# Late gates in single file, their stores issued by ScalarE, and the scan's first weights asked for at its opening

## The chip, the cores and the metric

One core of a Trainium2 chip runs the whole program. The metric is the device time of one execution in microseconds (us). The core has five engines that each work through their own list of instructions in order: PE (TensorE, the matrix unit), DVE (VectorE), ACT (ScalarE), POOL (GpSimd) and SP (SyncE, which here only issues DMAs). An engine waits where the next instruction of its list needs something that another engine or a DMA has not delivered; the instructions behind it wait too.

## The reference

One layer of a hybrid network: an FFN, a token mixer, and a second FFN, each with a layer norm. 128 context tokens and 1024 latent tokens (1152 in all, worked on as three column blocks of 384) with a width of 1024. The mixer makes one wide projection; its first columns feed a bidirectional recurrent branch with states (the scan), the next 512 a branch of centred means over windows of 2, 4, 8 and 16 tokens (pooling), and the last 2048 are the logits of two gates, which merge the branches:

```
proj = h @ p['w_mix_in']
ps = proj[..., :SHIFT_W]
pool_in = proj[..., SHIFT_W:SHIFT_W + D_B]
gate_logits = proj[..., SHIFT_W + D_B:]
...
s_final, y = lax.scan(_rwkv7_step, s0.astype(f32), xs)
...
y_a = y.astype(h.dtype) @ p['w_o_rwkv']
u = _centred_pool_residual(pool_in).reshape(b, t, POOL_GROUPS, POOL_GROUP_DIM)
u = jnp.einsum('btgc,gcd->btgd', u, p['w_pool']).reshape(b, t, D_B) * p['pool_scale']
y_b = u @ p['w_o_pool']
gate_a = jax.nn.sigmoid(gate_logits[..., :D_MODEL])
gate_b = jax.nn.sigmoid(gate_logits[..., D_MODEL:])
return (gate_a * y_a + gate_b * y_b) @ p['w_out'], s_final
```

## The kernel before

The program runs through stages: first FFN, the mixer's projections and preparations, the scan, the second FFN. The change lies where the projections end and the scan begins.

**Weights.** A product in float32 accuracy is made of three matmuls, of a high and a low half of each operand (L158 to L160). The class `Weights` fetches a weight block of 128x1024 by a DMA of SP into `wr` (two buffers), ACT casts it to the high half `wh` (L125), and DVE or POOL by turns subtracts to give the low half `wl` (L127); of the late gates the even ones have their `wl` from DVE, the odd ones from POOL. `wh` and `wl` have two buffers each here, so the cast for gate n waits until PE has read gate n-2.

**Late gates (L883 to L889).** Eight of the sixteen gate blocks, numbers 0 to 7, are made before the scan. Each has three column blocks b, each a gemm of 24 matmuls into PSUM, a sigmoid on ACT into `ga` (two buffers), and a store of 192 KB by SP into `gab`. The gates go in pairs: both gates' blocks 2 and 1 by turns, then both blocks 0. Each pair so needs the second gate's weights after two of its six gemms and frees the first gate's weights only after five.

**Beside them.** In the same part of the program two solves (`Solve`, index 0 and 1) prepare the scan: DVE works through 31 pairs of a multiply (L776, `pr`) and a subtraction (L778, `Wd`) and two transposes (L786 `Xi`, L787 `Yt`); of solve 0, PE then makes small products `ph` (L808) in the middle of the gates' matmuls, with copies on ACT (L802, L815 to L823). POOL and DVE make the pooling means (L905 to L911), stored as `u` by SP. The order of each engine's list here is made by the scheduler of the framework, from the program's text and its model of durations; so a change of the loop moves instructions on all engines.

**The scan's opening.** From `manual_schedule` on, the order is that of the text. Per step, PE makes `pa` (L1070) and `pt` (L1078), DVE masks `pa` to `LM` (L1072), ACT copies `pt` to `KBT` (L1080), then `xy`, `Xs`, `us`, `sp`. Into the gaps a generator, the filler, puts the rest of the gates and the pooling projection (`proj`, L936 to L940, and `pw`), one matmul at a time. Its weights come by `Halves`: loads of 128x512 by SP (L140, `wr<-in_w_pool`, `wr<-in_w_mix`), casts on ACT (L149), subtractions on POOL (L150). Its first two loads `uf` (L988) and its first weights are issued when the generator is first advanced, which is inside scan step 0, behind the loads of states (L1039), `ak` and `Gq`. The buffers of the scan stage lie where those of the late gates lay, so they come free with the last gates.

Of the kernel before, what the change touches and what calls it, by code (L numbers as in the profile page):

```python
# [9 lines left out]
F32 = mybir.dt.float32  # L10
# [7 lines left out]
P = 128  # L18
TAIL = 4
MODS = 3  # L20
EARLY = 8
# [14 lines left out]
BN = 384  # L36
# [25 lines left out]
def tile_step(ctx: ExitStack, tc: tile.TileContext, I: dict, O: dict):  # L62
    nc = tc.nc
    V, A, G, S, PE = nc.vector, nc.scalar, nc.gpsimd, nc.sync, nc.tensor
# [532 lines left out]
    with pool("mp", 4, psum=True) as psum, pool("ma", 2, psum=True) as paux, \  # L597
# [275 lines left out]
        with pool("m2") as pl:  # L873
            sols = [Solve(i) for i in range(9)]
            for k in range(22):
                sols[0].at(k)
            for k in range(13):
                sols[1].at(k)
            for s_, cs_ in enumerate(((0, 1), (1, 0), (2, 17))):
                load_ak(s_, cs_, 0)  # L880
            load_v(0, 0, (0, 1))
            load_v(1, 0, (2, 17))
            for n0 in range(0, EARLY, 2):  # L883
                for n, b in ((n0, 2), (n0, 1), (n0 + 1, 2), (n0 + 1, 1), (n0, 0), (n0 + 1, 0)):
                    ps = psum.tile([P, 512], F32, name="pm", tag="mm")
                    gemm(ps, W.get(27 + n), hs, b)
                    ga = pl.tile([P, 8, 64], F32, name="ga", tag="ga", bufs=2).rearrange("p h v -> p (h v)")[:, :BN]
                    A.activation(ga, ps[:, :BN], AF.Sigmoid)
                    S.dma_start(gab_d[n][b][:, 0, :], ga)  # L889
            for g, w in enumerate(WINDOWS):  # L890
                hw = w // 2
                base = (hw, TC + 3 * hw)
                invc = pl.tile([P, T], F32, name="invc", tag="invc", bufs=1)
                S.dma_start(invc, I["invc"][g].unsqueeze(0).broadcast_to([P, T]))
                pp = pl.tile([P, T + 32], F32, name="pp", tag="pp", bufs=1)
                G.memset(pp[:, 0:hw], 0.0)
                G.memset(pp[:, hw + TC:TC + 3 * hw], 0.0)
                G.memset(pp[:, T + 3 * hw:T + 4 * hw], 0.0)
                S.dma_start(pp[:, hw:hw + TC], pin_d[g][:, 0:TC])
                S.dma_start(pp[:, TC + 3 * hw:T + 3 * hw], pin_d[g][:, TC:])  # L900
                n, st, src = T + 4 * hw, 1, pp
                while st < w:
                    n -= st
                    dst = pl.tile([P, T + 32], F32, name="ws", tag="ws", bufs=2)
                    G.tensor_tensor(dst[:, :n], src[:, :n], src[:, st:st + n], ALU.add)  # L905
                    src = dst
                    st *= 2
                for o, ln, bs in ((0, TC, base[0]), (TC, T - TC, base[1])):
                    m = src[:, bs - hw:bs - hw + ln]
                    V.tensor_tensor(m, m, invc[:, o:o + ln], ALU.mult)  # L910
                    G.tensor_tensor(m, m, pp[:, bs:bs + ln], ALU.subtract)  # L911
                    S.dma_start(u_d[g][:, o:o + ln], m)
# [39 lines left out]
    def filler(psG):  # L952
        u = 0

        def nextw(look=2):
            nonlocal u
            u += 1
            return GW.get(u - 1, look)

        hh = hs[0]  # L960
        for b in range(NB):
            sl = slice(b * BN, (b + 1) * BN)
            if b:
                for n in (6, 7):
                    yield from back(*prev, n)
            u2 = [sg.tile([P, 4, BN], F32R, name="u2", tag=f"u2{k}", bufs=1) for k in range(2)]
            gts = {}

            def proj(n):
                ps = psG.tile([P, 512], F32, name="pm", tag="mm")  # L970
                for hf in range(2):
                    w = nextw()
                    yield from steps3(ps[:, :BN], [(w3(w[0], i), w3(w[1], i), hh[0][:, 4 * hf + i, :], hh[1][:, 4 * hf + i, :]) for i in range(4)],
                                      hf == 0, hf == 1)
                gts[n] = sg.tile([P, BN], F32, name="gt", tag="gt", bufs=3)
                A.activation(gts[n], ps[:, :BN], AF.Sigmoid)

            def back(b, u2, gts, n):
                w = nextw()
                ps = psG.tile([P, 512], F32, name="pb", tag="mm")  # L980
                yield from steps3(ps[:, :BN], [(w3(w[0], i), w3(w[1], i), u2[0][:, i, :], u2[1][:, i, :]) for i in range(4)])
                gt = gts.pop(n)
                V.tensor_tensor(gt, gt, ps[:, :BN], ALU.mult)
                later(gab_d[n][b][:, 1, :], gt)

            def load_u(g):
                t = sg.tile([P, BN], F32, name="uf", tag="uf", bufs=2)
                S.dma_start(t, u_d[g][:, sl])  # L988
                return t

            ufs = [load_u(0), load_u(1)]
            wp = nextw()
            first = chain(proj(0), proj(1))
            next(first)
            yield
            for g in range(4):
                uf = ufs[g]
                uh, ul = [sg.tile([P, BN], F32R, name="us", tag=f"us{k}", bufs=1) for k in range(2)]
                A.copy(uh, uf)
                G.tensor_tensor(ul, uf, uh.bitcast(F32), ALU.subtract)  # L1000
                for _ in range(PWGAP):
                    next(first)
                    yield
                ps = psG.tile([P, 512], F32, name="pw", tag="mm")
                yield from steps3(ps[:, :BN], [(w3(wp[0], g), w3(wp[1], g), uh, ul)])
                A.activation(uf, ps[:, :BN], AF.Copy, scale=pcol("pool_scale", g))
                split(uf, u2[0], u2[1], g, G)
                if g < 2:
                    ufs.append(load_u(g + 2))
            yield from first  # L1010
            for n in range(2, 8):
                yield from proj(n)
                if n == 7 and b < 2:
                    hh = [hpA.tile([P, KT, BN], F32R, name="hg", tag="hb") for k in range(2)]
                    for ks in (slice(0, 4), slice(4, 8)):
                        for k in range(2):
                            S.dma_start(hh[k][:, ks].bitcast(F32), h2_d[b + 1][k][:, ks])
                yield from back(b, u2, gts, n - 2)
            prev = (b, u2, gts)
        for n in (6, 7):  # L1020
            yield from back(*prev, n)

    with pool("s1") as pl, pool("gn") as gn, pool("spa", 2, psum=True) as psA, pool("spx", 1, psum=True) as psX, \
# [12 lines left out]
        def init_ctx(hb):  # L1036
            for d in range(2):
                G.memset(states[0, d], 0.0)
                S.dma_start(states[1, d], I["state"][d][:, 4 * hb:4 * hb + 4])  # L1039
# [164 lines left out]
        n = len(steps)  # L1204
        fl = filler(psG)
# [25 lines left out]
            fill(k)  # L1231

        with tc.manual_schedule(engines={PE.engine, V.engine, A.engine, G.engine, S.engine}):
            init_ctx(0)
            for s in range(3):
                pre(s)
                if s % 2 == 0:
                    load(s // 2)
            for s in range(2):
                for d in range(2 - s):  # L1240
                    pre_lm(s, d)
                    pre_kb(s, d)
            for s in range(n):
                if s == 18:
                    init_ctx(1)
                main(s)
                if s % 2 and s + 3 < n:
                    load((s + 3) // 2)
                if s + 1 < n:
                    pre_kb(s + 1, 1)  # L1250
                if s + 2 < n:
                    pre_lm(s + 2, 0)
                slot_work(s, 2)
                fill(2)
                if s + 2 < n:
                    pre_kb(s + 2, 0)
                hb, j = s // 18, s % 18
                if j == 1:
                    for d in range(2):
                        S.dma_start(O["st"][d][:, 4 * hb:4 * hb + 4], states[0, d])  # L1260
                for tt in range(9):
                    if (1 if tt == 0 else max(max(c, 19 - c) for c in (2 * tt, 2 * tt + 1))) == j:
                        waitgn.append(group_norm(hb, tt))
            while gns or waitgn:
                if waitgn:
                    gns.append(waitgn.pop(0))
                flush()
                drive(gns)
                for _ in range(10):
                    next(fl, None)  # L1270
            for _ in fl:
                pass
            flush()
# [177 lines left out]
```

## Time and profile before

| | us |
|---|---|
| median of 3 runs | 3419.12 |
| fastest, slowest of them | 3418.05, 3431.08 |
| the profiled execution | 3418.87 |
| its span in the trace | 3416.8 |
| PE busy in it | 3206.2 (94%) |
| DVE, ACT, POOL busy | 2002.7, 1187.2, 1308.0 |

The span runs from the first to the last instruction of the trace. PE's weight loads (PEld) overlap its matmuls. In lines of the timeline the bracket at the end is the idle time of that engine just ahead of the instruction, and what ended it; the releaser is inferred, and of several it is the latest one that the profile shows. PE's granted clock is given as a share of 2.4 GHz: 1.00 is that level, and 0.50 is the lower level of 1.2 GHz.

### The profile page before, as it was taken

To read this page: it belongs to the slowest core of one execution; us is meant where nothing else is said; L and a number is where in the kernel's file an instruction comes from. 1 tells how busy PE (TensorE), PEld (TensorE's weight loads), DVE (VectorE), ACT (ScalarE), POOL (GpSimd) and SP (SyncE) were. 2 spreads that over 40 slices of the span, in tenths; PEclk is the share of its full clock that TensorE was granted. 3 is DMA by queue.
4 is the path that set the end of the run, shared out by engine and by line. 5 is a ranking of instruction groups with operands and counts; after the bars stand their busy time and mean duration, and the time that the engine had idled before them with its cause. 6 is when DMAs were issued, how large, how long until landed. Compare 5 with 4: busy or idle time off the path is not lost.

```text
span 3416.8 us, 62644 instructions
## 1 busy us (share of the span) xinstructions
PE 3206.2 (94%) x25742; PEld 3044.4 (89%) x25742; DVE 2002.7 (59%) x3300; ACT 1187.2 (35%) x2006; POOL 1308.0 (38%) x1026
## 2 busy tenths in 40 slices
PE   7999999999999999888799889988999999999997
PEld 7999999999888888578688778878999999999996
DVE  6888633347537788866377777544574322323467
ACT  4111111125434444542255555544353111111133
POOL 5111211126446765754121452267763111111144
PEclk9999999999999999789899999999999999999998
DMA  6344211123455545556255566556541111111142
GB/s 238 131 137 137 91 44 38 50 75 130 170 171 161 171 151 160 159 167 206 89 176 163 173 189 210 167 165 222 201 154 38 38 49 38 50 38 45 55 134 95
DMA packets 271533, 433.29 MB, mean 127 GB/s; under 512 B 77840, under 2 KB 173584, under 8 KB 270224
## 3 DMA queue, kind: packets, MB, share of 16 engines
q1 hardware_dynamic: 271248, 429.30, 38.9%
q8 instruction: 202, 3.31, 0.4%
q14 instruction: 83, 0.68, 0.1%
HBM read 311.29 MB, written 96.53 MB: 119 GB/s over the span
## 4 chain that ended last, share of the span: by engine, by line
PE 60%; DVE 16%; DMA 9%; issue 5%; POOL 5%; ACT 3%; SPq 2%; DVEq 0%; POOLq 0%; ACTq 0%
PE pg L159 9%; PE pg L160 9%; PE pg L158 9%; PE po L159 4%; PE po L158 4%; PE po L160 4%; PE pm L158 2%; PE pm L160 2%; PE pm L159 2%; DVE wl L127 2%; PE pa L1070 2%; PE xy L1101 2%; DVE Wd L778 2%; DVE fm L403 2%; DVE pr L776 2%
## 5 line engine op out<-in xcount | busy, mean ns | idle before, releaser
L125 ACT CAST wh<-wr 128x1024 fp32r<-128x1024 f32 x270 | 280.5, 1049 | 800.9 <-PE po L159 432.6
L127 POOL TENSOR_TENSOR wl<-wr,wh 128x1024 fp32r<-128x1024 f32 x117 | 289.2, 2472 | 490.5 <-ACT wh L125 490.2
L295 POOL TENSOR_TENSOR gl<-sg,gh 128x384 fp32r<-128x384 f32 x132 | 157.6, 1194 | 784.0 <-ACT gh L294 784.0
L158 PE MATMUL po<-gh,wh 128*128 128x384 f32 x1056 | 357.3, 338 | 6.4 <-ACT gh L294 2.9
L159 PE MATMUL pg<-h1l,wh 128*128 128x384 f32 x1056 | 355.7, 337 | 7.5 <-POOL h1l L167 7.4
L159 PE MATMUL po<-gl,wh 128*128 128x384 f32 x1056 | 358.1, 339 | 3.6 <-POOL gl L295 3.6
L160 PE MATMUL po<-gh,wl 128*128 128x384 f32 x1056 | 356.4, 337 | 0.0
L158 PE MATMUL pg<-h1h,wh 128*128 128x384 f32 x1056 | 356.4, 337 | 0.0
L160 PE MATMUL pg<-h1h,wl 128*128 128x384 f32 x1056 | 354.5, 336 | 0.0
L158 PE MATMUL pg<-h3h,wh 128*128 128x384 f32 x1056 | 353.6, 336 | 0.0
L160 PE MATMUL pg<-h3h,wl 128*128 128x384 f32 x1056 | 353.5, 335 | 0.0
L159 PE MATMUL pg<-h3l,wh 128*128 128x384 f32 x1056 | 353.2, 335 | 0.0
L127 DVE TENSOR_TENSOR wl<-wr,wh 128x1024 fp32r<-128x1024 f32 x153 | 222.4, 1458 | 218.4 <-ACT wh L125 218.4
L160 PE MATMUL pm<-h2h,wl 128*128 128x384 f32 x936 | 328.2, 351 | 16.7 <-DVE wl L127 16.7
L292 DVE TENSOR_TENSOR sg<-sg,pg 128x384 f32<-128x384 f32 x132 | 73.0, 553 | 459.7 <-PE pg L160 453.6
L158 PE MATMUL pm<-h2h,wh 128*128 128x384 f32 x936 | 328.6, 351 | 0.9 <-ACT pads L442 0.9
L159 PE MATMUL pm<-h2l,wh 128*128 128x384 f32 x936 | 328.0, 350 | 0.0
L312 DVE SCALAR_TENSOR_TENSOR ac<-po,modh,ac 128x384 f32<-128x384 f32 (+1 forms) x352 | 172.9, 514 | 96.5 <-PE po L160 96.5
L403 DVE SCALAR_TENSOR_TENSOR fm<-fm 128x512 f32<-128x512 f32 x224 | 181.2, 809 | 54.7 <-DMA fm<-in_w_mod 51.5
L159 PEld LDWEIGHTS pg<-h1l,wh 128*128 128x128 f32 x1056 | 199.4, 189 | 10.9 <-POOL h1l L167 10.2
L158 PEld LDWEIGHTS po<-gh,wh 128*128 128x128 f32 x1056 | 199.6, 189 | 9.7 <-ACT gh L294 3.6
L160 PEld LDWEIGHTS pm<-h2h,wl 128*128 128x128 f32 x936 | 182.1, 195 | 24.0 <-DVE wl L127 17.3
(287 smaller groups left out, 7471.5 us busy)
## 6 DMA issues: line engine op xcount, KB each, us to landing
wr<-in_ffn_in SPq DMA_DIRECT2D x120, 512.0 KB
ak<-ak SPq DMA_DIRECT2D x48, 768.0 KB
ak<-ak SPq DMA_DIRECT2D x72, 512.0 KB
wr<-in_ffn_out SPq DMA_DIRECT2D x60, 512.0 KB
fm<-in_w_mod SPq DMA_DIRECT2D x112, 256.0 KB
wr<-in_w_mix SPq DMA_DIRECT2D x39, 512.0 KB
sh<-pads SPq DMA_DIRECT2D x108, 130.0 KB
wr<-in_w_mix SPq DMA_DIRECT2D x48, 256.0 KB
```

Source lines behind the costliest of these rows:

```text
L125: A.copy(h[:, :w], r[:, :w])
L127: e.tensor_tensor(l[:, :w], r[:, :w], h[:, :w].bitcast(F32), ALU.subtract)
L158: PE.matmul(ps, wh, xh, start=first and k == 0, stop=False)
L159: PE.matmul(ps, wh, xl, start=False, stop=False)
L160: PE.matmul(ps, wl, xh, start=False, stop=last and k == n - 1)
L292: lastv[0] = V.tensor_tensor(sg, sg, pu[:, :BN], ALU.mult)
L295: G.tensor_tensor(gs[j, b][1][:, sl], sg, gs[j, b][0][:, sl].bitcast(F32), ALU.subtract)
L312: lastv[0] = V.scalar_tensor_tensor(accs[b][:, n, s0:s1], po[:, s0:s1], modh[:, gate_i // 4, n, g:g + 1], accs[b][:, n, s0:s1], ALU.mult, ...
L403: V.scalar_tensor_tensor(jk, w, 1.0, silc[:, s, hf * 512:hf * 512 + 512], ALU.mult, ALU.mult, accum_out=part[:, kt, s, hf:hf + 1])
L776: V.tensor_tensor(o, Wd[:, 0:k + 1, k].unsqueeze(2).broadcast_to([P, k + 1, 31 - k]), Gq[:, k, k + 1:32].unsqueeze(1).broadcast_to([P, k + ...
L778: V.tensor_tensor(Wd[:, 0:k + 1, k + 1:32], Wd[:, 0:k + 1, k + 1:32], o, ALU.subtract)
L1070: PE.matmul(pa[e][:, i, :], ak[es, i, 128:256], ak[es, i, 0:128], start=True, stop=True)
```

## The change

Three edits. The late gates are listed in single file: gates 0 to 5 one after the other, each with its blocks 2, 1, 0, and only gates 6 and 7 still as a pair. The tile `ga` is [128, 384] with three buffers, where it was cut from a larger one with two, and its store is issued by ACT (`A`) where SP (`S`) issued it. The filler stops (`yield`) in its first pass once its first two `uf` loads and first weights are issued, and is advanced to that point ahead of the scan's first instructions.

```diff
@@ -880,13 +880,14 @@
             load_v(0, 0, (0, 1))
             load_v(1, 0, (2, 17))
-            for n0 in range(0, EARLY, 2):
-                for n, b in ((n0, 2), (n0, 1), (n0 + 1, 2), (n0 + 1, 1), (n0, 0), (n0 + 1, 0)):
+            late = [(n, b) for n in range(EARLY - 2) for b in (2, 1, 0)]
+            for n, b in late + [(n, b) for bs in ((2, 1), (0,)) for n in (EARLY - 2, EARLY - 1) for b in bs]:
+                if True:
                     ps = psum.tile([P, 512], F32, name="pm", tag="mm")
                     gemm(ps, W.get(27 + n), hs, b)
-                    ga = pl.tile([P, 8, 64], F32, name="ga", tag="ga", bufs=2).rearrange("p h v -> p (h v)")[:, :BN]
+                    ga = pl.tile([P, BN], F32, name="ga", tag="ga", bufs=3)
                     A.activation(ga, ps[:, :BN], AF.Sigmoid)
-                    S.dma_start(gab_d[n][b][:, 0, :], ga)
+                    A.dma_start(gab_d[n][b][:, 0, :], ga)
@@ -990,6 +991,8 @@
             ufs = [load_u(0), load_u(1)]
             wp = nextw()
+            if b == 0:
+                yield
             first = chain(proj(0), proj(1))
@@ -1231,6 +1234,7 @@
         with tc.manual_schedule(engines={PE.engine, V.engine, A.engine, G.engine, S.engine}):
+            next(fl)
             init_ctx(0)
```

The scheduler's lists show what moves. On DVE, at the start of solve 0, `wl_13927` is the low half of gate 2's weights before, `wl_13955` the same after; `pr` and `Wd` are the pairs of the solve, `ws` a pooling mean. Before:

```order
L127 TENSOR_TENSOR wl_13430<-wr_13427,wh_13429 128x1024
...
L776 TENSOR_TENSOR pr_13551<-Wd_13549,Gq_13540 128x31
...
L778 TENSOR_TENSOR Wd_13549<-Wd_13549,pr_13551 128x7x25
L776 TENSOR_TENSOR pr_13551<-Wd_13549,Gq_13540 128x8x24
L127 TENSOR_TENSOR wl_13927<-wr_13924,wh_13926 128x1024
L778 TENSOR_TENSOR Wd_13549<-Wd_13549,pr_13551 128x8x24
```

After:

```order
L127 TENSOR_TENSOR wl_13430<-wr_13427,wh_13429 128x1024
L911 TENSOR_TENSOR ws_14583<-ws_14583,invc_14575 128x128
L911 TENSOR_TENSOR ws_14583<-ws_14583,invc_14575 128x1024
L127 TENSOR_TENSOR wl_13955<-wr_13952,wh_13954 128x1024
L776 TENSOR_TENSOR pr_13551<-Wd_13549,Gq_13540 128x31
```

Gate 2's low half has moved ahead of the solve's first pair. In the same way gate 4's now stands inside solve 0, ahead of the pair 24x8 (before: behind solve 0's transposes), and gate 6's in the middle of solve 1, behind the pair 17x15 (before: ahead of its last pair). The pairs themselves keep their order. On PE the first products `ph` of solve 0 stand behind 12 gemms and 8 matmuls of the gates (296 matmuls), where they stood behind 11 gemms and 17 matmuls (281).

On SP, where the gates end and the scan opens (`Sc` are the states of the scan, `ak` operands of a later step, `Gq` and `Wd` those of solve 2). Before:

```order
L889 DMA gab_0_113<-ga 128x384
L889 DMA gab_0_116<-ga 128x384
L1039 DMA Sc_14683<-in_state 128x256
...
L862 DMA ak_14790<-ak_2_85 128x1024
L765 DMA Gq<-qd_0_1_162 16x1x1024 x2
...
L988 DMA uf<-u_191 128x384
L988 DMA uf<-u_192 128x384
L140 DMA wr<-in_w_pool 128x512
L140 DMA wr<-in_w_mix 128x512 x5
```

After:

```order
L913 DMA u_194<-ws 128x1024
L989 DMA uf<-u_191 128x384
L989 DMA uf<-u_192 128x384
L140 DMA wr<-in_w_pool 128x512
L140 DMA wr<-in_w_mix 128x512 x4
L1042 DMA Sc_14683<-in_state 128x256
...
L862 DMA ak_14818<-ak_2_85 128x1024
L765 DMA Gq<-qd_0_1_162 16x1x1024 x2
```

The stores of the gates are gone from SP, and the filler's loads stand ahead of the states, `ak` and `Gq`. The second `uf` load waits for the last matmul of gate 7, since its buffer lies where that gate's weights lay.

On ACT, in the same place. Before:

```order
L888 ACTIVATE ga<-pm 128x384 x7
L1080 COPY KBT_14709<-pt 128x512
L1080 COPY KBT_14729<-pt 128x512
L1080 COPY KBT_14749<-pt 128x512
L1111 COPY Xs<-xy 64x2x4x64 x2
L149 CAST wh<-wr 128x512 x4
```

After:

```order
L889 ACTIVATE ga<-pm 128x384
L890 DMA gab_0_113<-ga 128x384
L889 ACTIVATE ga<-pm 128x384
L890 DMA gab_0_116<-ga 128x384
L149 CAST wh<-wr 128x512 x3
L1083 COPY KBT_14737<-pt 128x512
L1083 COPY KBT_14757<-pt 128x512
L1083 COPY KBT_14777<-pt 128x512
L1114 COPY Xs<-xy 64x2x4x64 x2
L149 CAST wh<-wr 128x512
```

Each sigmoid is now followed by its store in ACT's own list, and three of the filler's casts stand ahead of the `KBT` copies. On POOL three of the subtractions L150 likewise stand ahead of the two memsets of the states (L1038 before). Each DMA issue, on either engine, also waits for an earlier DMA, since both take their completion semaphores by turns from the same eight: a store on ACT can so wait for a load that SP issued, and the other way round. At the passage from the scan to the second FFN a few loads, casts and subtractions also change places.

## Rows read from the trace of the kernel before

**Rows 1.** The windows view: each stretch's length, busy time of PE, PEld, DVE, ACT and POOL (with instructions), the granted clock, the DMA engines' busy share and GB/s.

```profile
1560.00:1580.00 20.00, 12.91 (x61) 12.91 (x62) 19.04 (x31) 2.09 (x5) 8.05 (x7) 0.74 0.92 313
...
1620.00:1640.00 20.00, 10.85 (x63) 10.53 (x62) 18.87 (x39) 3.48 (x5) 6.30 (x3) 0.84 0.16 59
...
1680.00:1700.00 20.00, 8.62 (x90) 7.17 (x92) 0.50 (x2) 6.16 (x9) 5.91 (x5) 0.57 0.59 163
```

**Rows 2.** The waits of PE from 1520 to 1720 us: what waited for what, us in total, times, the longest.

```profile
PE pm L160 <- DVE wl L127: 16.7, 2, 9.1
PE pm L936 <- ACT wh L149: 12.8, 1, 12.8
PE ph L808 <- DVE Yt L787: 2.0, 1, 2.0
PE pm L940 <- POOL wl L150: 0.9, 1, 0.9
```

**Rows 3.** The timeline of PE: start, duration, line, operation. First the wait for gate 2's low half, then `ph` of solve 0, then the wait for gate 6's low half, then the last gate's matmuls and the scan's opening.

```profile
1567.09 0.69 PE L160 MATMUL pm<-h2h,wl 128*128 128x384 f32 x1 [7.54 <-DVE wl L127]
...
1595.16 0.24 PE L808 MATMUL ph<-Yt,Nt 32*32 32x32 f32 x2 [2.03 <-DVE Yt L787]
...
1639.88 0.69 PE L160 MATMUL pm<-h2h,wl 128*128 128x384 f32 x1 [9.15 <-DVE wl L127]
...
1643.88 0.36 PE L160 MATMUL pm<-h2h,wl 128*128 128x384 f32 x1
...
1665.93 0.34 PE L160 MATMUL pm<-h2h,wl 128*128 128x384 f32 x1
1666.90 1.16 PE L1070 MATMUL pa<-ak 64*128 64x128 f32 x16 [0.63 <-ACT ga L888]
...
1673.49 2.00 PE L1101 MATMUL xy<-Sc,ak 64*128 64x64 f32 x32
...
1676.50 1.16 PE L1070 MATMUL pa<-ak 64*128 64x128 f32 x16
1690.48 0.69 PE L936 MATMUL pm<-h2h,wh 128*128 128x384 f32 x1 [12.82 <-ACT wh L149]
```

**Rows 4.** The timeline of DVE: solve 0's first pair, gate 2's low half, the subtraction of the pair 24x8 and the second transpose of solve 0, the subtraction of the pair 17x15 of solve 1, gate 6's low half, and the first pair of solve 2.

```profile
1556.00 0.19 DVE L776 TENSOR_TENSOR pr<-Wd,Gq 128x31 f32<-128x31 f32 x1 [23.05 <-ACT wh L125]
...
1565.82 1.22 DVE L127 TENSOR_TENSOR wl<-wr,wh 128x1024 fp32r<-128x1024 f32 x1
...
1586.37 0.36 DVE L778 TENSOR_TENSOR Wd<-Wd,pr 128x192 f32<-128x192 f32 x1
...
1593.23 1.88 DVE L787 STREAM_TRANSPOSE Yt<-Wd 128x1024 f32<-128x1024 f32 x1
...
1622.85 0.42 DVE L778 TENSOR_TENSOR Wd<-Wd,pr 128x255 f32<-128x255 f32 x1
...
1638.61 1.22 DVE L127 TENSOR_TENSOR wl<-wr,wh 128x1024 fp32r<-128x1024 f32 x1
...
1703.67 0.18 DVE L776 TENSOR_TENSOR pr<-Wd,Gq 128x31 f32<-128x31 f32 x1
```

**Rows 5.** The timeline of SP (issues of DMAs) from the last stores of the gates on.

```profile
1631.85 35.34 SPq L889 DMA_DIRECT2D gab<-ga  x8
...
1676.21 5.18 SPq L765 DMA_DIRECT2D Gq<-qd  x8
1681.43 0.92 SPq L988 DMA_DIRECT2D uf<-u  x2
1682.39 0.43 SPq L140 DMA_DIRECT2D wr<-in_w_pool  x1
```

**Rows 6.** The timeline of ACT and POOL at the scan's opening, and of SP and ACT where the scan ends (a load of 192 KB and the cast that waits for it).

```profile
1673.59 0.59 ACT L1080 COPY KBT<-pt 128x512 f32<-128x512 f32 x1 [1.80 <-PE pt L1078]
...
1689.14 2.61 ACT L149 CAST wh<-wr 128x512 fp32r<-128x512 f32 x4 [11.35 <-DMA wr<-in_w_pool]
...
1664.83 0.56 POOL L1038 MEMSET Sc<- 128x256 f32 x2 [30.98 <-DMA gab<-ga]
1689.83 4.96 POOL L150 TENSOR_TENSOR wl<-wr,wh 128x512 fp32r<-128x512 f32 x4 [24.44 <-ACT wh L149]
...
2276.45 0.54 SPq L1301 DMA_DIRECT2D gh<-gd_d  x1
...
2279.81 0.51 ACT L1302 CAST gh<-gh 128x384 fp32r<-128x384 f32 x1 [7.13 <-DMA gh<-gd_d]
```

**Rows 7.** The waits of ACT and of SP around the gates, and a sigmoid from ACT's timeline.

```profile
ACT ga L888 <- PE pm L160: 53.7, 13, 14.0
ACT ga L888 <- DMA gab<-ga: 18.7, 4, 10.2
...
SPq L889 <- ACT ga L888: 59.9, 15, 13.3
SPq L889 <- DMA ak<-ak: 1.7, 2, 1.3
...
1542.59 0.49 ACT L888 ACTIVATE ga<-pm 128x384 f32<-128x384 f32 x1 [3.67 <-PE pm L160]
```

**Rows 8.** The windows view of ten steps of the scan behind its opening (columns as in rows 1).

```profile
1720.00:1900.00 180.00, 170.58 (x3203) 153.73 (x3203) 134.95 (x271) 93.55 (x158) 38.38 (x30) 0.99 0.57 176
```

## The prediction

> **What bounds the kernel now.** I read the windows first, to find where PE is not busy, then PE's waits there, then the timelines of PE and of the engines it waits for. Over the scan's following steps PE is busy 170.58 of 180 us [rows 8], so what is late at the scan's opening is not caught up behind it, and what comes earlier there can be kept. Ahead of it lie the late gates and the opening, and there three windows of 20 us hold only 12.91, 10.85 and 8.62 us of PE work, at a granted clock of 0.74, 0.84 and 0.57 [rows 1]. The waits name the causes: 16.7 us in two waits for a `wl` of DVE, 12.8 us for one cast of the filler's weights, 2.0 us for `Yt`, 0.9 us for a subtraction of POOL [rows 2]. No engine is full here: it is order that bounds.
>
> In the timelines the first wait ends at 1567.09 (7.54 us) and the second at 1639.88 (9.15 us) [rows 3]. DVE made those two low halves at 1565.82 and 1638.61 [rows 4], the first behind pairs of solve 0 that began at 1556.00, the second at the end of solve 1. The third wait is a matter of SP: its last eight stores stretch over 35.34 us because each waits for its sigmoid [rows 5], and of SP's waits 59.9 us are for `ga` [rows 7]. Then came states, `ak` and 5.18 us of `Gq`, and only at 1682.39 the first weights [rows 5]. ACT could cast them at 1689.14, having waited 11.35 us [rows 6].
>
> **The change, part by part.** *Pace of the gates.* A sigmoid of 0.49 us behind a wait of 3.67 us [rows 7] says that one gemm takes 4.16 us at full clock, or 0.173 us for each of 24 matmuls. The sigmoid at 1542.59 is the second, so the gates begin at 1542.59 - 2 x 4.16 = 1534.3. They end at 1666.3 [rows 3].
>
> *Gate 2's low half* now stands ahead of solve 0, and gate 0 comes free after three gemms (1546.8) where it took five. Gate 2 is wanted after six, at 1559.3, and the subtraction takes 1.22 us [rows 4], so the wait of 7.54 us goes. But I do not count it as won, since `Yt` is late next. PE now reaches `ph` after 296 matmuls, 51.3 us, at 1585.6; gate 4's low half, now ahead of the pair 24x8, is ready about then (the pair's subtraction began at 1586.37, with one such subtraction ahead of it in either order [rows 4]), which costs perhaps 1 to 3 us and is swallowed. `Yt` is the end of DVE's own chain, which begins with a load at 1556.00 and runs without a gap; one low half of 1.22 us leaves that chain and another enters. So `ph` starts at 1595.16 as before, behind a new wait of some 7 to 9 us, where 7.54 and 2.03 us were. What is won is the 15 matmuls that now stand ahead of `ph`: 2.6 us. If DVE's chain moves by a few us, because POOL's pooling falls elsewhere, this term moves with it; I allow 4 us either way.
>
> *Gate 6's low half.* DVE makes it behind the pair 17x15, which ended at 1623.3 [rows 4], so by about 1624.6. Gate 6 begins six gemms, 25 us, before the gates' end; with the end at 1652.6 (below) that is 1627.7, a margin of 3 us. The wait of 9.15 us goes. So does the slow clock behind it: from 1639.88 to 1643.88 [rows 3] twelve matmuls took 4.0 us where 2.1 are due, 1.9 us. Bounds: all 11.0 us, or 8 if the margin is missed by 3.
>
> The gates then end at 1666.3 - 2.6 - 9.15 - 1.9 = 1652.6.
>
> *Stores on ACT.* 24 issues join ACT's list. No DMA issue by ACT is in the trace; SP's issue of a load took 0.43 us and of the two `uf` 0.46 each [rows 5]. 0.49 + 0.46 is under 1 us in a pace of 4.16, so PE covers it, unless the store has to wait. Two rows bound that wait: SP waited only 1.7 us in all for an `ak` load at its stores, but a sigmoid waited up to 10.2 us (18.7 in four) for a store to land [rows 7], in the stretch where the DMA engines were 92% busy [rows 1]. There are three `ga` buffers now and the gates' PSUM lets PE run ahead, so I take no cost; the upper bound is a rival below. Taking the stores off SP also frees SP to issue the loads of pooling and of gates' weights earlier; nothing on PE's path waits for those, so 0.
>
> On this stretch the Trainium skill speaks against the change: "DMA: Bandwidth & Descriptors", section "Issuing engines are not separate DMA queues", says that DMAs of whichever engine share the same 16 DMA engines, and that issuing from several saves only the sequencers' time. By it a store lands no sooner on ACT's queue, and the 18.7 us of waits for landing would stay, now in front of ACT's casts. The trace has no store on ACT to test it with; the first rival works out what that would come to.
>
> *The filler's weights.* They are asked for when the last gate's buffers are free, at 1652.6 + 0.9 for the two `uf`. A weight of 256 KB landed 6.75 us after its issue behind `Gq` (1682.39 to 1689.14 [rows 5, 6]), 192 KB in 3.36 us from an emptier queue (2276.45 to 2279.81 [rows 6]). I take 5, since nothing large is ahead: 1658.5, three casts of 0.65 us and three subtractions of 1.24 us [rows 6] by about 1662 to 1663. Before, PE did 10.8 us of scan work between the gates' end and its wait (1666.90 to 1677.7 [rows 3]), which now runs from 1653.2 to 1664.0; the weights are there by then. So 12.8 and 0.9 us of waits go [rows 2], and with the idle time some of the slow clock behind it: PE's 8.62 us in that window, at 0.57 [rows 1], would be 4.9 at full clock, 3.7 less. I take 2.2, since part of the work is small and waits for other engines; the bounds are 0 and 3.7.
>
> *What it pushes back.* The three casts stand ahead of the `KBT` copies and the three subtractions ahead of POOL's memset of the states, which `xy` needs 6.6 us after the opening (1673.49 - 1666.90 [rows 3]). The memset would end at 1653.2 + 6.6 = 1659.8 without cost; behind subtractions that end between 1660.3 and 1663.6 (landing 3.4 or 6.75) and with 0.56 us of its own it ends 1.0 to 4.3 us late. I take 2.6. `Gq` of solve 2 moves behind the weights, but solve 2 began only at 1703.67 [rows 4], 27 us behind its `Gq`; that slack covers it. At the passage to the second FFN I take 0, with 3 us either way.
>
> **The sum.** 2.6 + 9.15 + 1.9 + 12.8 + 0.9 + 2.2 - 2.6 = 27.0. From the profiled execution's 3418.87 us: 3391.9, call it 3392. The median of the runs, 3419.12, is a quarter of a microsecond off, which I neglect. The terms' bounds (4 for `Yt`, 3 for gate 6, 2 each for the clock and for what is pushed back, 3 at the passage) add, taken as independent, to some 6: 3386 to 3398. What a measurement can tell from no change is about 0.5%, 17 us: 3402 to 3436 counts as the same.
>
> **The rivals.** *Half of it is hidden anyway (A).* The stores wait for landings as before, ACT's casts come late, and the second wait at a `wl` is replaced by one for a cast; the gates end as before and only the opening is won: 3418.9 - 12.8 - 0.9 + 2.6 = 3408. For it: the 18.7 us of landing waits and the slim margin at gate 6. Against: they fell in the one stretch with full DMA engines; from 1620 on these were 16% busy [rows 1].
>
> *The weights come no earlier relative to the scan (B).* They cannot start before the last gate ends, and their casts and subtractions stand in the way of `KBT` and the states; if landing takes 10 us and more, the opening loses what it wins and only the gates' 13.65 us stay: 3405. Against: 13 us of the old wait came from issues queued ahead, which the row of SP shows [rows 5].
>
> *ACT becomes the bound (C), the slower side.* Each store blocks ACT's list until an earlier DMA lands. If every one did so for 6.75 us, a gemm costs 0.49 + 0.43 + 6.75 = 7.7 us on ACT, 24 of them 184, and the gates end at 1718, 52 us late; less 13.7 at the opening: 3457. It is even from a wait of 5.2 us on ((1666.3 + 13.7 - 1534.3) / 24 = 6.1 us a gemm) and slower by 0.5% from 5.9 us. For it: the mean of the four landing waits, 4.7 us. Against: only 4 of 24, and at SP's stores 1.7 us in all.
>
> *All is won (D).* `Yt` comes 4 us earlier, nothing is pushed back: 3392 - 4 - 2.6 = 3385, and to 3381 with more clock.
>
> **How the numbers follow.** Forecast 0.55, D 0.10, A 0.13, B 0.10, C 0.07, and 0.05 for something that gives no change or a little loss. Faster by over 0.5% are the forecast, D and a good fifth of A and B: 0.70; the same: the rest of A and B and most of the remainder, 0.22; slower: C and a little, 0.08. The range leaves out the far side of D and all of C: 3379 to 3412.
>
> **What would show it.** Right: PE waits for neither gate 2's nor gate 6's `wl`; a wait for `Yt` of 7 to 9 us ends near 1595; the gates end near 1653; the filler's first load is issued a microsecond later and PE's `pm` L936 waits less than 2 us; the scan's windows are the old ones, 27 us earlier. Wrong: sigmoids or casts on ACT that wait for DMAs of more than 5 us on average (C), a wait of PE for an ACT cast within the gates (A), `xy` over 5 us late on the states' memset (B), or a scan whose own steps grow.

## The result, and the profile after

The changed kernel takes 3397.88 us (median of 6 runs, 3388.34 to 3403.25), the kernel before 3418.48 on the same chips. The ratio is 0.9936 with a 95% interval from 0.9923 to 0.9949: 0.6% faster, some 21 us, where 27 were forecast. The profiled execution of the changed kernel took 3397.27 us, its span is 3395.5.

Its windows, at four of the places read before (columns as in rows 1; the gates begin 2.5 us later in this execution):

```profile
1560.00:1580.00 20.00, 20.00 (x117) 20.00 (x116) 18.83 (x38) 3.97 (x6) 6.01 (x7) 1.00 1.03 363
1580.00:1600.00 20.00, 10.79 (x56) 10.08 (x55) 18.02 (x27) 5.12 (x6) 8.68 (x5) 0.79 0.26 86
1620.00:1640.00 20.00, 20.00 (x117) 20.00 (x117) 19.04 (x35) 3.42 (x6) 6.05 (x4) 1.00 0.22 81
1660.00:1680.00 20.00, 18.53 (x243) 16.55 (x239) 5.47 (x10) 10.95 (x19) 6.27 (x8) 0.83 0.51 159
```

The two windows that held 12.91 and 10.85 us of PE work [rows 1] are full at full clock. One new gap has opened between 1580 and 1600, and the opening, now in the last window, is almost full. PE's waits from 1520 to 1710 us:

```profile
PE ph L808 <- DVE Yt L787: 7.0, 1, 7.0
PE pm L160 <- DVE wl L127: 2.2, 1, 2.2
PE xy L1104 <- POOL Sc L1041: 1.5, 1, 1.5
```

So of the 32.4 us of waits [rows 2] those for the filler's cast and subtraction and both long waits for a low half are gone, and 10.7 us stand at places where there were 2.0. Where they stand, in PE's timeline:

```profile
1589.18 0.45 PE L160 MATMUL pm<-h2h,wl 128*128 128x384 f32 x1 [2.18 <-DVE wl L127]
...
1597.56 0.31 PE L808 MATMUL ph<-Yt,Nt 32*32 32x32 f32 x2 [7.03 <-DVE Yt L787]
...
1654.70 1.16 PE L1073 MATMUL pa<-ak 64*128 64x128 f32 x16 [0.58 <-ACT ga L889]
...
1662.91 3.30 PE L1104 MATMUL xy<-Sc,ak 64*128 64x64 f32 x32 [1.47 <-POOL Sc L1041]
1666.14 1.97 PE L1110 MATMUL xy<-vu,LM 64*64 64x64 f32 x32
```

The first is gate 4's low half, the second the new wait for `Yt`. Against 2.5 us of later start, `ph` begins at the same time as before (1595.16 in rows 3). The third wait, of 1.5 us, looks small; but the same `xy` of 32 small matmuls took 2.00 us before [rows 3] and takes 3.30 here. The windows view of the stretch behind the wait shows PE at its lower clock (0.50, the last figure but two):

```profile
1663.50:1670.00 6.50, 6.50 (x74) 6.09 (x72) 0.00 (x0) 1.79 (x4) 0.00 (x0) 0.50 0.45 147
```

DVE shows why the waits in the gates stand where they do: gate 2's low half is out early, gate 6's in time, and the solve's chain still has its slow steps of some 2.2 us.

```profile
1550.16 1.23 DVE L127 TENSOR_TENSOR wl<-wr,wh 128x1024 fp32r<-128x1024 f32 x1 [14.74 <-ACT wh L125]
...
1580.11 2.21 DVE L778 TENSOR_TENSOR Wd<-Wd,pr 128x231 f32<-128x231 f32 x1
1582.36 2.20 DVE L776 TENSOR_TENSOR pr<-Wd,Gq 128x220 f32<-128x220 f32 x1
...
1595.61 1.89 DVE L787 STREAM_TRANSPOSE Yt<-Wd 128x1024 f32<-128x1024 f32 x1
...
1625.20 1.22 DVE L127 TENSOR_TENSOR wl<-wr,wh 128x1024 fp32r<-128x1024 f32 x1
```

On ACT the stores take 0.33 us each to issue, and some wait first for an earlier DMA; here are three of them, each with the sigmoid behind it, and at the end the filler's first cast. SP issued that weight at 1654.56, 28 us earlier than before [rows 5].

```profile
1558.90 0.34 ACTq L890 DMA_DIRECT2D gab<-ga  x1
1559.29 0.49 ACT L889 ACTIVATE ga<-pm 128x384 f32<-128x384 f32 x1 [5.38 <-DMA Nt<-nd]
...
1571.82 0.33 ACTq L890 DMA_DIRECT2D gab<-ga  x1
1572.25 0.49 ACT L889 ACTIVATE ga<-pm 128x384 f32<-128x384 f32 x1 [5.98 <-DMA vu<-vt]
...
1574.80 0.33 ACTq L890 DMA_DIRECT2D gab<-ga  x1
1575.18 0.49 ACT L889 ACTIVATE ga<-pm 128x384 f32<-128x384 f32 x1 [2.43 <-DMA wr<-in_w_mix]
...
1658.19 0.62 ACT L149 CAST wh<-wr 128x512 fp32r<-128x512 f32 x1 [3.54 <-DMA wr<-in_w_pool]
```

The first and the third of these stores waited for a load of SP, `Nt` and `wr`. At the second the bracket misleads: by the trace's semaphore records the store itself had waited until 1571.75, when ACT's own store of 1564.38 landed, 7.4 us after its issue, and `vu` is only the last landing that the profile shows ahead of the sigmoid.

To compare runs I use three stretches, since the gates' start itself lies anywhere between 1528 and 1539 us over the profiles of this study, with the same code ahead of it. Each row is read from one profiled execution. The stretches are the gates (from 4.16 us ahead of the first sigmoid to the scan's first `pa`), the opening (from there to the first copy `yt`), and the passage to the second FFN (from the filler's last `pm<-hg` that waits for over a microsecond to the `pm<-yh` with the longest wait for ACT's `yh`).

| us | gates | opening | passage | median |
|---|---|---|---|---|
| before | 132.6 | 33.9 | 46.9 | 3418.5 |
| changed | 117.9 | 21.5 | 50.8 | 3397.9 |
| stores on SP again | 118.0 | 23.8 | 50.2 | 3397.1 |
| without early weights | 118.3 | 32.7 | 46.2 | 3404.6 |
| only early weights | 134.1 | 23.8 | 50.2 | 3410.6 |
| only stores on ACT | 129.2 | 34.1 | 50.2 | 3417.1 |
| `ph` later | 114.0 | 21.6 | 50.0 | 3393.6 |
| memset first | 117.6 | 16.9 | 50.1 | 3392.8 (one run) |
| low half on DVE | 118.3 | 21.8 | 49.1 | 3395.4 |
| no window sums | 115.2 | 21.5 | 50.3 | 3384.9 (one run, work left out) |
| the edits together | 114.3 | 16.9 | 47.5 | 3389.5 |
| `ph` later still | 112.1 | 16.9 | 49.5 | 3377.9 |

### The profile page after: what moved, and what is told of

It is laid out like the page before. It is cut to its first block, busy times and chain, and to the rows that moved or that the text cites. A ratio compares the mean times of both kernels' runs of the same rounds, so it can differ in the third digit from the quotient of the medians.

```text
span 3395.5 us, 62626 instructions
## 1 busy us (share of the span) xinstructions
PE 3209.4 (95%) x25742; PEld 3049.6 (90%) x25742; DVE 2007.4 (59%) x3300; ACT 1185.9 (35%) x2006; POOL 1306.5 (38%) x1026
## 4 chain that ended last, share of the span: by engine, by line
PE 64%; DVE 15%; DMA 8%; issue 5%; POOL 4%; ACT 3%; SPq 1%; DVEq 0%; POOLq 0%; ACTq 0%
PE pg L159 8%; PE pg L160 8%; PE pg L158 8%; PE po L159 5%; PE po L158 5%; PE po L160 5%; PE pm L158 4%; PE pm L159 4%; PE pm L160 3%; DMA fm<-in_w_mod 2%; DVE fm L403 2%; PE pa L1073 2%; PE xy L1104 2%; DVE wl L127 1%; PE ph L808 1%
## 5 line engine op out<-in xcount | busy, mean ns | idle before, releaser
L403 DVE SCALAR_TENSOR_TENSOR fm<-fm 128x512 f32<-128x512 f32 x224 | 182.6, 815 | 53.3 <-DMA fm<-in_w_mod 50.3
L159 PEld LDWEIGHTS po<-gl,wh 128*128 128x128 f32 x1056 | 199.3, 189 | 4.1 <-POOL gl L295 4.1
```

The source lines that it names most:

```text
L159: PE.matmul(ps, wh, xl, start=False, stop=False)
L403: V.scalar_tensor_tensor(jk, w, 1.0, silc[:, s, hf * 512:hf * 512 + 512], ALU.mult, ALU.mult, accum_out=part[:, kt, s, hf:hf + 1])
```

## The experiments

**Which edit does what.** Four runs take the change apart.

The first, on the changed kernel:

```diff
-                    A.dma_start(gab_d[n][b][:, 0, :], ga)
+                    S.dma_start(gab_d[n][b][:, 0, :], ga)
```

> The changed kernel with one edit undone: the gates' stores are issued by SP again. Theory (the order of the gates and of the weights does it all, the move of the stores to ACT is worth nothing by itself): the gates end within 3 us of the changed kernel's (117.3 us after their start), the only losses being gate 6's low half, which DVE has three pairs later, and a last store ahead of the filler's weights; the whole time 3398 to 3402. Rival (SP's queue, held up by stores that wait for sigmoids, was what delayed weights and the opening): the gates end 5 us or more later, or the wait at L937 comes back with 5 us or more; 3405 to 3412.

Measured 3397.1 us (ratio 0.9946, 0.9925 to 0.9966), with the gates at 118.0 and the opening at 23.8. The theory holds: the move of the stores to ACT is worth 2.4 us in these two stretches, which the medians do not show. With the stores on SP the sigmoids waited 16.0 us for stores to land and PE 2.6 us for a sigmoid, in place of the 2.2 us for gate 4's low half; the wait for `Yt` (7.1 us) swallowed that.

The second, on the changed kernel:

```diff
-            if b == 0:
-                yield
...
-            next(fl)
             init_ctx(0)
```

> The changed kernel without the early stop of the filler: the gates in single file and their stores on ACT are kept. Theory (the two gains add): the gates end 117 us after their start as in the changed kernel, then PE waits some 12 to 13 us at L936 for the first cast, as in the kernel before, since states, ak and Gq stand ahead of the weights again; 3409 to 3413. Rival (with no stores on SP the weights come early anyway): the wait is under 6 us; 3400 to 3405.

Measured 3404.6 us (0.9964, 0.9942 to 0.9986). The stretches are as the theory has them: gates 118.3, and the wait at L937 is back to a hundredth.

```profile
1681.30 0.69 PE L937 MATMUL pm<-h2h,wh 128*128 128x384 f32 x1 [12.83 <-ACT wh L149]
...
1683.20 0.69 PE L941 MATMUL pm<-h2h,wl 128*128 128x384 f32 x1 [0.90 <-POOL wl L150]
```

The median is 4 us under the expected range, and its profiled execution, 3410.2, inside it. This run's passage takes 46.2 us and not 50.8, to which the third group of runs returns.

The third, on the kernel before:

```diff
             wp = nextw()
+            if b == 0:
+                yield
...
+            next(fl)
             init_ctx(0)
```

> The kernel before with only the early stop of the filler. Theory (the two gains add): both waits for a low half of DVE stay (16 to 17 us), the gates end 132 us after their start, the wait at L936 goes; 13 us faster than before, 3404 to 3407. Rival (the early weights pay only where the stores are off SP): the weights' issues are still stuck behind the last stores and the wait shrinks by half at most; 3411 to 3416.

Measured 3410.6 us (0.9981, 0.9969 to 0.9994), between the two. The wait at L936 is gone and the opening is 10.1 us shorter, so the weights pay without the other edits; but the gates took 1.5 us more and the passage 3.3 more. PE's long waits in the gates are the old ones:

```profile
1568.29 0.69 PE L160 MATMUL pm<-h2h,wl 128*128 128x384 f32 x1 [8.87 <-DVE wl L127]
...
1641.05 0.69 PE L160 MATMUL pm<-h2h,wl 128*128 128x384 f32 x1 [9.10 <-DVE wl L127]
```

The fourth, on the kernel before:

```diff
-                    ga = pl.tile([P, 8, 64], F32, name="ga", tag="ga", bufs=2).rearrange("p h v -> p (h v)")[:, :BN]
+                    ga = pl.tile([P, BN], F32, name="ga", tag="ga", bufs=3)
                     A.activation(ga, ps[:, :BN], AF.Sigmoid)
-                    S.dma_start(gab_d[n][b][:, 0, :], ga)
+                    A.dma_start(gab_d[n][b][:, 0, :], ga)
```

> The kernel before with only the stores on ACT and three ga buffers; gates in pairs, weights late. Theory (nothing by itself): the scheduler makes gate 6's low half six pairs earlier on DVE, so the second wait shrinks by 2 to 4 us, the rest stays; 3414 to 3418. Rival (the stores on ACT cost: waits for earlier DMAs in ACT's list delay casts): the gates end later than 132 us after their start; 3420 to 3430. Second rival (SP set free is worth much): 3408 or less.

Measured 3417.1 us (0.9998, 0.9987 to 1.0009): nothing by itself, as the theory has it. The gates are 3.4 us shorter, though gate 6's wait hardly shrank (8.84 us for 9.15); the passage is 3.3 us longer.

**What now ends last, in the gates and at the opening.** On the changed kernel, the steps of solve 0 from the placing of its blocks on are written into the list after 14 gemms:

```diff
-            for k in range(22):
+            for k in range(13):
                 sols[0].at(k)
...
+                if (n, b) == (4, 0):
+                    for k in range(13, 22):
+                        sols[0].at(k)
```

> The changed kernel with the steps of solve 0 from the placing of its blocks on written into the list after 14 gemms of the gates: PE reaches ph 43 matmuls (7.5 us) later in its list. Theory (the wait of 7.0 us for Yt is on PE's path, and DVE's chain sets it): ph still starts some 61 us after the gates' start, now behind a wait under 1 us; the slow clock behind it goes too, perhaps 2 us; gate 5's low half, whose cast stands behind solve 0's copies on ACT, may be 1 to 3 us late; the gates end 6 to 9 us earlier after their start (109 to 112 us against 117.9), the time is 3390 to 3393. Rival (something else ends last in the gates, gate 5's or gate 6's low half): the wait moves there and the gates end within 3 us of the changed kernel's.

Measured 3393.6 us (0.9931, 0.9914 to 0.9947), the gates 114.0: 3.9 us won where 6 to 9 were expected. `ph` still began 60.3 us after the gates' start (60.8 in the changed kernel), so DVE's chain does set it. But PE met three small waits in place of the long one:

```profile
1591.24 0.24 PE L808 MATMUL ph<-Yt,Nt 32*32 32x32 f32 x2 [2.08 <-DVE Yt L787]
1592.70 0.21 PE L808 MATMUL ph<-Wb,Nt 32*32 32x32 f32 x1 [1.22 <-ACT Wb L802]
...
1627.81 0.45 PE L160 MATMUL pm<-h2h,wl 128*128 128x384 f32 x1 [1.07 <-POOL wl L127]
```

The rival (the wait moves on) takes a part of it: gate 7's low half is the last.

On the changed kernel, the states' memsets of the first half go ahead of the filler:

```diff
-                G.memset(states[0, d], 0.0)
+                if hb:
+                    G.memset(states[0, d], 0.0)
...
+            for d in range(2):
+                G.memset(states[0, d], 0.0)
             next(fl)
```

> The changed kernel with the two memsets of the states ahead of the filler's first subtractions in POOL's list. Theory (what the early weights push back is xy, through POOL): the wait of 1.5 us of xy for Sc goes, and the first yt comes 1.5 us earlier after the opening (20.0 against 21.5 us). Rival (the KBT copies behind the casts on ACT hold PE anyway): a wait of 1 us or more for KBT takes its place, and the first yt stays at 21 to 21.5.

The opening shrank from 21.5 to 16.9 us, by 4.6 where 1.5 was expected. The wait is gone, and with it the slow clock behind it:

```profile
1659.76 2.00 PE L1105 MATMUL xy<-Sc,ak 64*128 64x64 f32 x32
1661.70 1.15 PE L1111 MATMUL xy<-vu,LM 64*64 64x64 f32 x32
```

These two took 3.30 and 1.97 us in the changed kernel (its timeline above). So 1.5 us of waiting cost 3.1 us more in slower matmuls. No wait for `KBT` came in its place.

**The passage.** The changed kernel and the five variants above with a long passage (50.0 to 50.8) share one order of POOL's list there, and the two with a short one (before, and without early weights: 46.9, 46.2) share another: with no line of the passage edited, the scheduler had put a subtraction of 128x1024 ahead of the last group norm's `y`. POOL's timeline in the changed kernel, and then PE's, waiting for it:

```profile
2290.45 1.27 POOL L150 TENSOR_TENSOR wl<-wr,wh 128x512 fp32r<-128x512 f32 x1
2291.69 2.36 POOL L127 TENSOR_TENSOR wl<-wr,wh 128x1024 fp32r<-128x1024 f32 x1
2294.01 2.02 POOL L1185 TENSOR_TENSOR y<-y,gvr 128x512 f32<-128x512 f32 x1
```

```profile
2296.09 1.12 PE L1193 MATMUL pt<-cst,y 128*128 128x128 f32 x4 [2.84 <-POOL y L1185]
2296.85 0.67 PE L939 MATMUL pb<-u,wh 128*128 128x384 f32 x1
2297.32 0.52 PE L941 MATMUL pb<-u,wl 128*128 128x384 f32 x1
```

The 0.52 us is the lower clock again. The test moves this one subtraction:

```diff
-        W = Weights(wpool, pun, look=2, raw=2, hl=2, eng="pv", more=wmore)
+        W = Weights(wpool, pun, look=2, raw=2, hl=2, eng="vv" + "pv" * 40, more=wmore)
```

> The changed kernel with one subtraction of 128x1024 moved: the low half of the second FFN stage's first weight is made by DVE and not by POOL, so POOL's list has no subtraction ahead of the last group norm's y at the passage from the scan. Theory (the reordering there gives back 3 to 4 us of the gain): the stretch from PE's last filler wait (pm<-hg) to its first matmul of yh shrinks from 50.8 to 47 to 48 us, and the time is 3394 to 3396. Rival (the passage is bound by the group norm's chain, and the order of one subtraction is no matter): the stretch stays at 50 to 51 us.

Measured 3395.4 us (0.9938, 0.9923 to 0.9953), the passage 49.1. PE's wait there fell from 2.84 to 0.97 us, but did not vanish, since the step of POOL ahead of it grew while DVE ran the subtraction. POOL's timeline in this run, and then DVE's:

```profile
2286.53 2.63 POOL L1183 TENSOR_TENSOR gvr<-gvr,half 128x8 f32<-128x8 f32 x1
2289.14 1.27 POOL L150 TENSOR_TENSOR wl<-wr,wh 128x512 fp32r<-128x512 f32 x1
2290.37 2.02 POOL L1185 TENSOR_TENSOR y<-y,gvr 128x512 f32<-128x512 f32 x1
```

```profile
2285.80 1.86 DVE L127 TENSOR_TENSOR wl<-wr,wh 128x1024 fp32r<-128x1024 f32 x1 [1.44 <-ACT wh L125]
```

`gvr` took 2.63 where the changed kernel's last two took 1.64 and 1.65. In this run the move so gives back 1.7 of the 3.9 us. Most of the rest is the new collision of the two engines, as the run with the edits together (below) shows: it holds the same move, but there DVE's subtraction began behind `gvr` (2281.12 against 2280.92), neither step of POOL grew, and the passage took 47.5 us, 3.3 less than in the changed kernel:

```profile
2280.92 1.64 POOL L1186 TENSOR_TENSOR gvr<-gvr,half 128x8 f32<-128x8 f32 x1
2282.53 1.28 POOL L150 TENSOR_TENSOR wl<-wr,wh 128x512 fp32r<-128x512 f32 x1
2283.77 1.04 POOL L1188 TENSOR_TENSOR y<-y,gvr 128x512 f32<-128x512 f32 x1
```

```profile
2281.12 1.23 DVE L127 TENSOR_TENSOR wl<-wr,wh 128x1024 fp32r<-128x1024 f32 x1 [2.38 <-ACT wh L125]
```

In the last run below they grew again (2.63 and 2.02), and the passage took 49.5. What the other moved entries cost (two casts on ACT ahead of `yo`, loads on SP) was not tried.

**Why `Yt` is late.** On the changed kernel, POOL's running sums are skipped:

```diff
-                while st < w:
+                while st < w and g < 0:
```

> The changed kernel without the running sums of the pooling windows on POOL (the pooled means are left out of the result; loads, scaling and stores stay). Theory (DVE's pairs of a solve take 2 us in place of 0.4 while POOL runs a wide tensor_tensor, and this lengthens the chain to Yt): no pair of solve 0 is slow beside a sum, its 31 pairs take 29 to 32 us to the second transpose's start where they take 36.9, and PE's wait for Yt shrinks from 7.0 to 0 to 3 us. Rival (the slow pairs have another cause, the DMA traffic): four or five pairs of solve 0 stay at 2 us, the chain at 35 us or more.

From its first pair to the second transpose solve 0 took 33.6 us (1552.84 to 1586.39) in place of 36.9: shorter by 3.3, not by the 5 to 8 expected, and PE's wait for `Yt` stayed at 6.6, since PE lost most of its wait at gate 4 too (0.4 us is left of 2.2) and came 2.6 us earlier. The chain got new losses in this run: inside it DVE waited 0.8 and 1.4 us for DMAs ahead of two scalings of the pooling (L911), and gate 4's low half took 2.92 us for 1.22, beside a POOL step. But the cause of the slow steps is shown. The one instruction of the pairs that stayed slow lies beside POOL's subtraction, as the timelines of DVE and of POOL show:

```profile
1562.21 2.51 DVE L776 TENSOR_TENSOR pr<-Wd,Gq 128x252 f32<-128x252 f32 x1
```

```profile
1562.05 2.40 POOL L127 TENSOR_TENSOR wl<-wr,wh 128x1024 fp32r<-128x1024 f32 x1 [13.71 <-ACT wh L125]
```

All others ran at 0.2 to 0.45 us, as they do before where POOL is idle. In the changed kernel the three slow instructions from 1580.11 on run beside POOL's sums, which are as long as they are:

```profile
1579.88 2.19 POOL L906 TENSOR_TENSOR ws<-pp 128x1167 f32<-128x1167 f32 x1 [11.53 <-DMA pp<-pin]
1582.15 4.39 POOL L906 TENSOR_TENSOR ws<-ws 128x1165 f32<-128x1165 f32 x2
```

Each of these DVE instructions ends 0.2 to 0.3 us behind the POOL instruction beside which it began. The Trainium skill has it as a rule ("SBUF — State Buffer", section "Who interferes with whom"): a DVE instruction with two inputs in SBUF contends with a GpSimd instruction that reads SBUF, since the ports that the two share are an exclusive lock. The trace agrees, with 2.2 us for 0.4.

**Together.** The edits of the three gains at once, and gates 6 and 7 in single file as well:

```diff
-            late = [(n, b) for n in range(EARLY - 2) for b in (2, 1, 0)]
-            for n, b in late + [(n, b) for bs in ((2, 1), (0,)) for n in (EARLY - 2, EARLY - 1) for b in bs]:
-                if True:
+            for n, b in [(n, b) for n in range(EARLY) for b in (2, 1, 0)]:
+                if (n, b) == (4, 0):
+                    for k in range(13, 22):
+                        sols[0].at(k)
```

> The changed kernel with three edits that showed a gain each: solve 0's ph 43 matmuls later, the states' memset ahead of the filler's subtractions, the second FFN stage's first low half on DVE; and gates 6 and 7 in single file too, so that gate 7's low half is wanted 4.2 us later. Theory (each wait stands on PE's path and they add): the gates end 112 to 114 us after their start, the first yt comes 16.5 to 17.5 us after the opening, the passage takes 48.5 to 49.5 us, the time is 3383 to 3389. Rival (the waits hide one another, what is gained at one place is waited for at the next): the sum of these stretches shrinks by under 5 us against the changed kernel's, the time stays at 3391 to 3396.

Measured 3389.5 us (0.9913, 0.9885 to 0.994), just above what was expected: gates 114.3, opening 16.9, passage 47.5, so 11.5 us less than the changed kernel in the three. The rival as it was put (under 5 us) is out. But not all of it arrives in this profile: the scan between opening and passage took 591.5 us where the changed kernel's took 585.3, and at the first `lnv` of the layer norm behind the passage 5.4 us are left. The next section returns to the scan.

The last differs from it by one number:

```diff
-                if (n, b) == (4, 0):
+                if (n, b) == (5, 2):
```

> As the run beside it, with ph one gemm (24 matmuls, 4.2 us) later still, behind three matmuls of gate 5. Theory (gate 5's low half, cast by ACT behind the copies of Yt, is what ends last then): no wait for Yt, but a wait of 3 to 5 us at gate 5's low half in its place, and the gates end within 2 us of the run beside it. Rival (only Yt held PE): the gates end 2 to 4 us earlier than in the run beside it.

Measured 3377.9 us (0.9889, 0.9872 to 0.9907), the fastest of the study. No wait for `Yt` is left, and the one at gate 5 is 1.2 us where 3 to 5 were expected:

```profile
PE pm L160 <- DVE wl L127: 2.6, 1, 2.6
PE pm L160 <- POOL wl L127: 1.2, 1, 1.2
```

The gates end 2.2 us earlier than in the run beside it, which is the rival's figure: mostly `Yt` had held PE. The three stretches sum to the same 178.5 and 178.7 us in the two runs, and the intervals of their ratios overlap; that the medians lie 11 us apart is not explained by what was edited. Of the 9.4 us between the two profiles' spans 3.8 lie in the gates' start (1528.1 and 1531.8), 3.7 in the scan (587.8 and 591.5) and 1.8 behind the first `lnv`.

## Why the prediction was right, and by how much it was off

The time fell in the range, on the forecast's side; each of its mechanisms was there, and the gain was over-estimated by 6 us.

*The gates:* 13.65 us forecast, 14.7 measured (132.6 to 117.9). Both waits for a low half went, and the step "`Yt` is late next" was right in place and size: 7.03 us of the 7 to 9, ending where it had ended before. Gate 4's low half cost 2.2 us ahead of it, swallowed as forecast. That the wait for `Yt` is on the path the run with `ph` later shows.

*The opening:* 13.3 forecast, 12.4 measured (33.9 to 21.5). The waits of 12.8 and 0.9 us went, and returned to a hundredth without the early weights. A weight landed 3.6 us after its issue where 5 were taken. The term that was mis-sized is what is pushed back: 2.6 us were taken, 4.6 came back when the memset went first. I had counted the lateness of the memset and not what PE's clock does behind it. The term for the clock behind the old wait was too small in turn: with the memset first the opening is 17.0 us shorter than before, where the terms without what is pushed back give 15.9.

*Stores on ACT at no cost:* right. ACT's list waited up to 6.0 us for a DMA at a store, and in all its brackets name 16.9 us of such waits at sigmoids, near the 18.7 of before [rows 7]; but those waits were covered, and the gates took no longer than with the stores on SP (117.9, 118.0). Of rival C the mechanism was there and the price was not: from 1582 on sigmoids wait for PE, not for DMAs. Rival A named the same waits and is out, since PE waited for no cast within the gates; rival B was half of a truth, the part that the memset run measured.

*The passage at 0, with 3 us either way:* here the step failed. The stretch grew by 3.9 us, of which about 1.5 came back by the first `lnv` of the layer norm behind it. I had seen that loads, casts and subtractions change places there and did not ask which list has the last link: POOL's, with one subtraction ahead of the group norm's `y`. All seven profiles with that order have a passage 3.1 to 3.9 us longer than the kernel before, whichever of the edits they hold.

*What arrives at the end:* 27.1 us are won up to the first `yt` (166.5 to 139.4 from the gates' start), just what the sum said, though in part by luck: the gates gave 1.0 us and the clock at the opening 1.1 more than their terms, and what is pushed back took 2.0 more. 25.4 are left where the filler last waits for `hg`, 21.5 behind the passage and 23.0 at `lnv`. The 1.7 us went within the 36 steps of the scan, which the change does not edit. The windows view of that stretch, before and then changed:

```profile
1700.81:2284.39 583.58, 537.51 (x9858) 483.54 (x9858) 408.25 (x808) 321.96 (x569) 201.59 (x161) 0.97 0.57 176
1676.21:2261.47 585.26, 540.00 (x9859) 485.51 (x9859) 404.97 (x808) 321.86 (x569) 201.24 (x161) 0.97 0.58 177
```

PE was busy 2.5 us longer in it with the same matmuls. The trace's clock records hold 29.5 us of the stretch at 0.50 before and 38.3 in the changed kernel. Over the twelve profiles of this study it takes from 581.7 us (31.8 at 0.50) to 591.5 (44.8, the run with the edits together), and mostly longer where more of it ran at the lower level. Why the clock fell more often is not shown. So a few microseconds between two runs can come from the scan alone, and the stretches say more of an edit than the time of its run. The gates began 2.5 us late in the profiled execution, by chance as far as the other profiles tell.

## What to carry to other kernels

Where an engine waits for a result, ask what the next late result is before counting the wait as won: here 7.5 us of one wait became 7 us of another, and only the second wait of the pair paid. Price an edit also at places that it does not touch, if a scheduler orders them: compare the order at every seam, and look for one instruction put ahead of a chain's last link. And a load that is merely asked for late was the cheapest thing to move here, provided that nothing which the first step needs is pushed behind its casts.

## What the runs showed of the hardware

A wait of 1.5 us at the opening, with only small matmuls just ahead of it, went with PE's lower clock, and the matmuls behind it lost 3.1 us more. I had looked for that behind the long waits alone. It is no single case: in the six profiles that have this wait for `Sc` (1.2 to 1.6 us) the 32 matmuls of `xy` behind it took 2.9 to 3.7 us, in the six that have not they took 2.00, and the three with the memset first are among these. Nor does every such wait bring it: in the run with the edits together PE waited 1.3 us for DVE's `Sc` at a later `pt` (1678.85), and from 1678 to 1690 its granted clock stayed at 1.00.

A store issued by a compute engine can wait, in that engine's own list, for a load that another engine issued, because both count on the same completion semaphores: 5.4 us for `Nt` and 2.4 us for `wr` in the changed kernel. It can wait for its own engine's earlier store as well, 6.0 us in one place. That it cost nothing I put down to PE's 4.16 us a gemm and to the PSUM tiles into which PE can run ahead; with fewer of these it was not tried.
